# Seven buffers in place of three for the embedding terms of the gate

## The chip, the core and the metric

The kernel runs on one core of a Trainium2 chip. The core has a matrix engine (TensorE, PE in the profile; its weight loads are PEld), a vector engine (VectorE, DVE), an activation engine (ScalarE, ACT), a general engine (GpSimd, POOL) and a queue engine (SyncE, SP), which here issues the DMA transfers. Each engine works through its instructions in the order in which they are written for it, and semaphores hold an instruction until what it needs is there. SBUF is the on-chip memory for tiles, PSUM the memory (in banks) that TensorE writes. The metric is the time of one execution in microseconds; lower is better.

## What is computed

One layer of a hybrid encoder on 1024 positions of width 1024. The part around the change is the end of it:

```python
mixed = jnp.concatenate([attn, conv_out], axis=-1) @ w_out[i]
x = x + rms_norm(mixed, post_norm_gain[i])
e = rms_norm(p[i] @ w_ple_proj[i], ple_norm_gain[i])
x = x + jax.nn.sigmoid(x @ w_ple_gate[i]) * e
```

`attn` is block-causal differential attention in four heads, `conv_out` a gated short convolution; both come from one projection of the normalised input.

## The kernel before

All activations lie transposed, as tiles of 128 channels by 512 positions: `kt` or `m` counts the 8 channel tiles, `n` the two halves of the positions. Each product is done in three passes of split operands (a high and a low part, lines 100 to 102), so that a tile of the output projection or the gate takes 8 x 3 = 24 matmuls of 512 columns.

The products e = p @ w_ple_proj are made at the start and stored to DRAM (`e_dram`). Projections, attention heads and convolutions follow. The last stage works on `mT` (the split copy of the concatenated result) with the 8 tiles of `w_out`, then on `x1` (the split copy of the new residual) with the 8 tiles of `w_gate`. A weight tile is loaded (`load_w`, line 124), cast by ScalarE into its high part and reduced by GpSimd to its low part (both in `split`, lines 89 and 90; the GpSimd instruction is called a split below). `out_half(m, n)` makes one tile of the output projection, and ScalarE copies it and squares it; VectorE adds the squares (line 523). `post` scales the result and adds x. `gate_half(m, n)` makes one tile of the gate. It loads the tile of e (line 550), scales it by gain and norm (line 551), takes tanh of the matmul result (line 560), and VectorE joins both in two instructions (lines 561 and 562) that write into the buffer of e. That buffer is then stored to the output (line 563). The last call, (7,1), does its matmuls and what follows in two pieces of 256 columns.

The gate's 16 tiles are made in the order (0,0) to (5,0), (0,1) to (5,1), (6,0), (6,1), (7,0), (7,1), written (m,n). The buffers of e come from the pool `c4` under the tag `e`. A buffer can be loaded again when the store that reads it has landed. Results of TensorE go to banks from two groups in turn, `p` with two banks and `s` with three.

The order on each engine is made by a scheduler when the kernel is built, from the program's text, its dependencies and its buffers. The pools of the last stage lie in memory that the stages before have left, so a larger pool also moves its neighbours, and what a tile of the last stage waits for can change with its place. The pool `c4` is opened before `wp2`, which holds five of the eight weight tiles.

The last projection tile of the convolutions (`pj`, emptied by lines 424 and 432) comes just before the output projection; line 427 and 428 finish the convolution's gate, line 287 a head's result.

Of the kernel before, what the change touches and what calls it, by code (L numbers as in the profile page):

```python
# [12 lines left out]
F32 = mybir.dt.float32  # L13
# [7 lines left out]
P = 128  # L21
# [4 lines left out]
HALF = 512  # L26
# [17 lines left out]
def hybrid_layer(ctx, tc, xT, pT, w_in, small, lams, w_out, w_ple, w_gate, outT):  # L44
# [18 lines left out]
    def bank_s(name):  # L63
        return ps_s.tile([P, HALF], F32, tag="s", bufs=3, name=name)

    def bank_p(name):
        return ps_s.tile([P, HALF], F32, tag="p", bufs=2, name=name)
# [16 lines left out]
    def col(base, k):  # L84
        return sm[:, base + k:base + k + 1]

    def split(hi, lo, src, scale=None, lo_eng=None):
        if scale is None:
            A.copy(out=hi, in_=src)  # L89
            (lo_eng or V).tensor_tensor(out=lo, in0=src, in1=hi.bitcast(F32), op=sub)  # L90
        else:
            return (A.activation(out=hi, in_=src, func=AF.Copy, scale=scale),
                    V.scalar_tensor_tensor(out=lo, in0=src, scalar=scale, in1=hi.bitcast(F32), op0=mult, op1=sub))

    def rsqrt(out, ssq, n, eps):
        V.tensor_scalar(out=out, in0=ssq, scalar1=1.0 / n, scalar2=eps, op0=mult, op1=add)
        G.tensor_tensor(out=out, in0=out, in1=nhalf[:, :ssq.shape[-1]], op=ALU.pow)
# [7 lines left out]
    def column_sums(acc, pool, extra=None, tag="flip"):  # L105
        flip = pool.tile([P, HALF], F32, tag=tag, name="flip")
        V.transpose(out=flip, in_=acc)
        part = tiny.tile([P, 32], F32, tag="part", name="part")
        V.tensor_reduce(out=part[:, 0:16], in_=flip.rearrange("p (f r) -> p f r", r=32), axis=AX.X, op=add)
        if extra is not None:  # L110
            V.tensor_tensor(out=part[:, 16:32].rearrange("p (t f) -> p t f", t=4),
                            in0=extra.unsqueeze(2).broadcast_to([P, 4, 4]),
                            in1=own.unsqueeze(1).broadcast_to([P, 4, 4]), op=mult)
        n = 16 if extra is None else 32
        ms = bank_t("ms")
        T.matmul(out=ms[:, :n], lhsT=fold, rhs=part[:, :n], start=True, stop=True)
        return ms

    def spread(out, row):
        V.transpose(out=out, in_=row.unsqueeze(2).broadcast_to([P, 16, 32]))  # L120

    def load_w(src, pool=None, lo_eng=G):
        raw = rawp.tile([P, KT, P], F32, tag="raw", name="raw")
        nc.sync.dma_start(out=raw, in_=src)
        w = (pool or wp).tile([P, 2, KT, P], F32R, tag="w", name="w")
        split(w[:, 0], w[:, 1], raw, lo_eng=lo_eng)
        return w

    def product(w, rhs, n, bank):
        for kt in range(KT):  # L130
            b = rhs[n][kt]
            mm3(bank, w[:, 0, kt], w[:, 1, kt], b[:, 0], b[:, 1], kt == 0, kt == KT - 1)
        return bank

    def operand(name):
        return [[hp.tile([P, 2, HALF], F32R, tag="H", name=f"{name}{n}_{kt}") for kt in range(KT)] for n in range(2)]
# [349 lines left out]
    with ExitStack() as st:  # L486
        cp = st.enter_context(tc.tile_pool(name="cp", bufs=1, reuse_waits="tile"))
        c2 = st.enter_context(tc.tile_pool(name="c2", bufs=2, reuse_waits="tile"))
        c4 = st.enter_context(tc.tile_pool(name="c4", bufs=4, reuse_waits="tile"))
        wp2 = st.enter_context(tc.tile_pool(name="wp2", bufs=5, reuse_waits="tile"))  # L490

        order = [(w_out, m) for m in range(KT)] + [(w_gate, m) for m in range(KT)]
        tiles = {}

        def weight(k):
            if k not in tiles:
                src, m = order[k]
                tiles[k] = load_w(src[m], pool=wp if k % KT in (1, 4, 7) else wp2)
            return tiles[k]

        banks = [0]

        def bank():
            banks[0] += 1
            return bank_p("o") if banks[0] % 2 else bank_s("o")

        mT = operand("mT")
        for n in range(2):
            for kt in range(KT):
                split(mT[n][kt][:, 0], mT[n][kt][:, 1], mix[kt][n])  # L510

        accs = [None, None]

        def out_half(m, n):
            ps = product(weight(m), mT, n, bank())
            A.copy(out=mix[m][n], in_=ps)
            if m == 0:
                accs[n] = cp.tile([P, HALF], F32, name=f"acc{n}")
                A.activation(out=accs[n], in_=ps, func=AF.Square)
            else:  # L520
                sq = c2.tile([P, HALF], F32, tag="sq", name="sqo")
                A.activation(out=sq, in_=ps, func=AF.Square)
                V.tensor_tensor(out=accs[n], in0=accs[n], in1=sq, op=add)

        x1 = None

        def post_stat(n):
            r = tiny.tile([P, 16], F32, tag="rs", name="rso")
            rsqrt(r, column_sums(accs[n], cp)[:, :16], D, 1e-6)
            return r  # L530

        def post(n, r):
            S1 = accs[n]
            spread(S1, r)
            for kt in range(KT):
                o = mix[kt][n]
                xt = c4.tile([P, HALF], F32, tag="xt", bufs=3, name="xt")
                nc.sync.dma_start(out=xt, in_=xT[n, kt])
                V.scalar_tensor_tensor(out=o, in0=o, scalar=col(C_POST, kt), in1=S1, op0=mult, op1=mult)  # L539
                (G if kt else V).tensor_tensor(out=o, in0=o, in1=xt, op=add)  # L540
                split(x1[n][kt][:, 0], x1[n][kt][:, 1], o)

        re = []

        def gate_half(m, n):
            if len(re) == n:
                re.append(cp.tile([P, HALF], F32, name=f"re{n}"))
                spread(re[n], rs_e[:, 16 * n:16 * n + 16])
            e = c4.tile([P, HALF], F32, tag="e", bufs=3, name="e")
            nc.sync.dma_start(out=e, in_=e_dram[n, m])  # L550
            V.scalar_tensor_tensor(out=e, in0=e, scalar=col(C_PLE, m), in1=re[n], op0=mult, op1=mult)  # L551
            w = weight(KT + m)
            pieces = 2 if (m, n) == (KT - 1, 1) else 1
            step = HALF // pieces
            for c0 in range(0, HALF, step):
                c, o = slice(c0, c0 + step), slice(n * HALF + c0, n * HALF + c0 + step)
                ps = bank()[:, :step]
                product(w, [[b[:, :, c] for b in r] for r in x1], n, ps)
                t = c2.tile([P, HALF], F32, tag="tg", name="tg")[:, :step]
                A.activation(out=t, in_=ps, func=AF.Tanh, scale=0.5)  # L560
                V.scalar_tensor_tensor(out=e[:, c], in0=t, scalar=1.0, in1=e[:, c], op0=add, op1=mult)
                V.tensor_tensor(out=e[:, c], in0=e[:, c], in1=mix[m][n][:, c], op=add)
                nc.sync.dma_start(out=outT[m * P:(m + 1) * P, o], in_=e[:, c])

        for m in range(KT):
            out_half(m, 0)
        r = post_stat(0)
        out_half(0, 1)
        x1 = operand("x1")
        post(0, r)  # L570
        for m in range(1, KT):
            out_half(m, 1)
        r = post_stat(1)
        gate_half(0, 0)
        post(1, r)
        for m in range(1, 6):
            gate_half(m, 0)
        for m in range(0, 6):
            gate_half(m, 1)
        for m in range(6, 8):  # L580
            gate_half(m, 0)
            gate_half(m, 1)
# [37 lines left out]
```

## Time and profile before

| | |
|---|---|
| median of 3 runs | 652.25 us (650.86 to 652.95) |
| the profiled execution | 651.04 us |
| its span in the trace | 649.3 us |
| VectorE busy | 447.8 us, 69% of the span |
| ScalarE busy | 243.7 us, 38% |
| GpSimd busy | 227.0 us, 35% |

The span runs from the first to the last profiled instruction of one execution. The executions shown differ among themselves by up to 2.1 us. Times in the trace count from the span's start.

### The profile page before, as it was taken

To read this page: it belongs to the slowest core of one execution; us is meant where nothing else is said; L and a number is where in the kernel's file an instruction comes from. 1 tells how busy PE (TensorE), PEld (TensorE's weight loads), DVE (VectorE), ACT (ScalarE), POOL (GpSimd) and SP (SyncE) were. 2 spreads that over 40 slices of the span, in tenths; PEclk is the share of its full clock that TensorE was granted. 3 is DMA by queue.
4 is the path that set the end of the run, shared out by engine and by line. 5 is a ranking of instruction groups with operands and counts; after the bars stand their busy time and mean duration, and the time that the engine had idled before them with its cause. 6 is when DMAs were issued, how large, how long until landed. Compare 5 with 4: busy or idle time off the path is not lost.

```text
span 649.3 us, 8064 instructions
## 1 busy us (share of the span) xinstructions
PE 631.8 (97%) x2941; PEld 523.2 (81%) x2941; DVE 447.8 (69%) x821; ACT 243.7 (38%) x442; POOL 227.0 (35%) x114
## 2 busy tenths in 40 slices
PE   7899999999999999999999999999999999999992
PEld 4688888888888888888888888888888888888882
DVE  6968512698786687876886999539881199795233
ACT  6945312334463333543444434114632326231110
POOL 2006100325326544256362132424560379450000
PEclk9999999999999999999999999999999999999997
DMA  8976522310254102352012400113140125143222
GB/s 286 383 279 194 195 86 86 92 58 5 82 145 138 44 34 81 103 158 65 33 49 82 130 33 33 65 34 130 65 163 0 34 73 187 33 145 98 93 86 97
DMA packets 35654, 67.77 MB, mean 104 GB/s; under 512 B 3744, under 2 KB 12448, under 8 KB 35616
## 3 DMA queue, kind: packets, MB, share of 16 engines
q1 hardware_dynamic: 35616, 67.27, 31.5%
q8 instruction: 23, 0.38, 0.2%
q14 instruction: 15, 0.12, 0.1%
HBM read 48.38 MB, written 12.58 MB: 94 GB/s over the span
## 4 chain that ended last, share of the span: by engine, by line
PE 71%; DVE 12%; DMA 9%; ACT 3%; issue 2%; POOL 2%; DVEq 0%; POOLq 0%; ACTq 0%
PE pj L100 14%; PE pj L102 14%; PE pj L101 14%; PE s L237 5%; DMA e<-e_dram 4%; DMA out_dram<-e 3%; DVE mix L539 3%; PE o L102 3%; PE o L100 3%; PE o L101 3%; PE tpw L264 2%; PE v L100 2%; PE v L101 2%; PE v L102 2%; DVE x L90 2%
## 5 line engine op out<-in xcount | busy, mean ns | idle before, releaser
L100 PE MATMUL pj<-hT,w 128*128 128x512 f32 x448 | 176.4, 394 | 1.2 <-ACT w L89 1.2
L101 PE MATMUL pj<-hT,w 128*128 128x512 f32 x448 | 176.2, 393 | 0.0
L102 PE MATMUL pj<-hT,w 128*128 128x512 f32 x448 | 176.1, 393 | 0.0
L90 POOL TENSOR_TENSOR w<-raw,w 128x1024 fp32r<-128x1024 f32 x41 | 105.5, 2582 | 146.6 <-ACT w L89 143.8
L100 PEld LDWEIGHTS pj<-hT,w 128*128 128x128 f32 x448 | 84.2, 188 | 18.1 <-ACT w L89 2.0
L102 PEld LDWEIGHTS pj<-hT,w 128*128 128x128 f32 x448 | 84.2, 188 | 16.4
L101 PEld LDWEIGHTS pj<-hT,w 128*128 128x128 f32 x448 | 84.2, 188 | 16.1
L245 ACT ACTIVATE p<-p,nm 128x128 f32<-128x128 f32 (+7 forms) x64 | 49.4, 772 | 70.6 <-DVE nm L241 60.7
L89 ACT CAST w<-raw 128x1024 fp32r<-128x1024 f32 x44 | 45.9, 1048 | 21.2 <-issue 11.6
L102 PE MATMUL o<-x,w 128*128 128x512 f32 (+1 forms) x136 | 51.3, 377 | 0.0
L100 PE MATMUL o<-x,w 128*128 128x512 f32 (+1 forms) x136 | 51.2, 377 | 0.0
L101 PE MATMUL o<-x,w 128*128 128x512 f32 (+1 forms) x136 | 51.2, 377 | 0.0
L100 PE MATMUL o<-mT,w 128*128 128x512 f32 x128 | 49.8, 389 | 0.0
L101 PE MATMUL o<-mT,w 128*128 128x512 f32 x128 | 49.8, 389 | 0.0
L102 PE MATMUL o<-mT,w 128*128 128x512 f32 x128 | 49.7, 390 | 0.0
L237 PE MATMUL s<-ks,qs 128*128 128x512 f32 (+2 forms) x192 | 47.5, 346 | 0.0
L89 ACT CAST wt<-tpw 128x512 fp32r<-128x512 f32 (+3 forms) x48 | 21.1, 479 | 60.1 <-PE tpw L264 60.0
L90 DVE TENSOR_TENSOR wt<-tpw,wt 128x512 fp32r<-128x512 f32 (+3 forms) x48 | 25.3, 551 | 26.2 <-ACT wt L89 26.1
L551 DVE SCALAR_TENSOR_TENSOR e<-e,small_c,re 128x512 f32<-128x512 f32 x16 | 16.3, 1017 | 36.5 <-DMA e<-e_dram 36.5
L241 DVE CUSTOM_DVE_ANT_0 p<-s,bias 128x512 f32<-128x512 f32 (+3 forms) x64 | 34.8, 564 | 9.3 <-PE s L237 5.4
L237 PEld LDWEIGHTS s<-ks,qs 128*128 128x128 f32 x192 | 33.4, 188 | 5.0
L405 POOL TENSOR_TENSOR mix<-mix,R 128x512 f32<-128x512 f32 x8 | 12.3, 1543 | 68.6 <-DVE mix L404 66.4
(139 smaller groups left out, 1117.6 us busy)
## 6 DMA issues: line engine op xcount, KB each, us to landing
raw<-in_w_in SPq DMA_DIRECT2D x32, 512.0 KB, 3.6
mix<-in_xT SPq DMA_DIRECT2D x16, 256.0 KB, 6.6
e_dram<-e SPq DMA_DIRECT2D x16, 256.0 KB, 5.6
mix<-e_dram SPq DMA_DIRECT2D x16, 256.0 KB, 3.1
ks<-ks SPq DMA_DIRECT2D x16, 256.0 KB, 3.5
v_dram<-v SPq DMA_DIRECT2D x8, 512.0 KB, 2.6
vs<-v_dram SPq DMA_DIRECT2D x32, 128.0 KB, 2.7
raw<-in_w_out SPq DMA_DIRECT2D x8, 512.0 KB, 3.2
```

The source lines that it names most:

```text
L89: A.copy(out=hi, in_=src)
L90: (lo_eng or V).tensor_tensor(out=lo, in0=src, in1=hi.bitcast(F32), op=sub)
L100: T.matmul(out=ps, lhsT=ah, rhs=bh, start=first, stop=False)
L101: T.matmul(out=ps, lhsT=ah, rhs=bl, start=False, stop=False)
L102: T.matmul(out=ps, lhsT=al, rhs=bh, start=False, stop=last)
L237: T.matmul(out=banks[m][:, :nn], lhsT=s.qs[:, m, qi], rhs=s.ks[:, m, part, c], start=part == 0, stop=part == 1)
L241: V.tensor_tensor_reduce(out=pr[m][:, c0:c0 + n], in0=banks[m][:, :n], in1=s.bias[:, b0:b0 + n], scale=-1.0, scalar=low[m], op0=add, op1=A ...
L245: A.activation(out=pr[m][:, :W], in_=pr[m][:, :W], func=AF.Exp, scale=-1.0, bias=low[m], accum_out=l[:, m:m + 1])
L264: T.transpose(out=tp[:, ii * P:(ii + 1) * P], in_=s.ws[ii][:, j * P:(j + 1) * P], identity=ident)
L405: G.tensor_tensor(out=o, in0=o, in1=R[n], op=mult)
L539: V.scalar_tensor_tensor(out=o, in0=o, scalar=col(C_POST, kt), in1=S1, op0=mult, op1=mult)
L551: V.scalar_tensor_tensor(out=e, in0=e, scalar=col(C_PLE, m), in1=re[n], op0=mult, op1=mult)
```

## The change

The pool's tag `e` gets seven buffers of 128 x 512 in place of three. Nothing is added or taken out; the built program has the same instructions in another order.

```diff
--- before.py
+++ after.py
@@ -546,7 +546,7 @@
             if len(re) == n:
                 re.append(cp.tile([P, HALF], F32, name=f"re{n}"))
                 spread(re[n], rs_e[:, 16 * n:16 * n + 16])
-            e = c4.tile([P, HALF], F32, tag="e", bufs=3, name="e")
+            e = c4.tile([P, HALF], F32, tag="e", bufs=7, name="e")
             nc.sync.dma_start(out=e, in_=e_dram[n, m])
             V.scalar_tensor_tensor(out=e, in0=e, scalar=col(C_PLE, m), in1=re[n], op0=mult, op1=mult)
             w = weight(KT + m)
```

What the scheduler makes of it shows at two places. The first is where the last stage begins. On VectorE the subtractions `mT1_k` (the low parts of the second half of mT) are line 90, line 432 empties the last projection tile `pj`, and the `e` tiles are e_4765 for (0,0), e_4852 for (1,0) and so on. Lines with - are of before, with + of the changed program:

```order
 L90 TENSOR_TENSOR mT1_3_4141<-mix3_1_117,mT1_3_4141 128x512
+L90 TENSOR_TENSOR mT1_4_4142<-mix4_1_119,mT1_4_4142 128x512
+L90 TENSOR_TENSOR mT1_5_4143<-mix5_1_121,mT1_5_4143 128x512
 L432 TENSOR_TENSOR mix7_1_125<-pj_4087,mix7_1_125 128x512
-L90 TENSOR_TENSOR mT1_4_4142<-mix4_1_119,mT1_4_4142 128x512
-L551 SCALAR_TENSOR_TENSOR e_4765<-e_4765,small_c_78,re0_4763 128x512
-L90 TENSOR_TENSOR mT1_5_4143<-mix5_1_121,mT1_5_4143 128x512
-L551 SCALAR_TENSOR_TENSOR e_4852<-e_4852,small_c_78,re0_4763 128x512
 L90 TENSOR_TENSOR mT1_6_4144<-mix6_1_123,mT1_6_4144 128x512
 L90 TENSOR_TENSOR mT1_7_4145<-mix7_1_125,mT1_7_4145 128x512
```

Two subtractions move ahead of line 432, and the scalings of line 551, which stood between them, move behind the last of the subtractions, where there are now six in a row. On ScalarE at the same place, w_4180, w_4247 and w_4281 are the high parts of w_out's tiles 0, 2 and 3, and line 425 is the tanh of the last convolution gate:

```order
 L89 CAST mT0_7_4137<-mix7_0_124 128x512
+L89 CAST w_4180<-raw_4178 128x1024
+L89 CAST w_4247<-raw_4245 128x1024
+L89 CAST w_4281<-raw_4279 128x1024
 L425 ACTIVATE ty_4081<-y_4080 128x512
 L89 CAST mT1_0_4138<-mix0_1_111 128x512
```

These three casts stood behind mT1_3 before. A little later on ScalarE, w_4315, w_4349 and w_4383 are the tiles 4, 5 and 6, and lines 516 and 519 copy and square the first tile of the output projection:

```order
 L89 CAST mT1_5_4143<-mix5_1_121 128x512
+L89 CAST w_4315<-raw_4313 128x1024
 L89 CAST mT1_6_4144<-mix6_1_123 128x512
+L89 CAST w_4349<-raw_4347 128x1024
 L89 CAST mT1_7_4145<-mix7_1_125 128x512
-L89 CAST w_4315<-raw_4313 128x1024
+L516 COPY mix0_0_110<-o_4183 128x512
+L519 ACTIVATE acc0_4209<-o_4183 128x512
+L89 CAST w_4383<-raw_4381 128x1024
```

Two casts have moved ahead of the cast of mT1_7, and that of w_4383 stands behind it.

The second place is the gate, here on VectorE: e_5143 is (3,1), e_5176 is (4,1), e_5209 is (5,1), e_5242 is (6,0), e_5280 is (6,1) and e_5351 is (7,1), the last tile:

```order
 L561 SCALAR_TENSOR_TENSOR e_5143<-tg_5171,e_5143 128x512
-L551 SCALAR_TENSOR_TENSOR e_5209<-e_5209,small_c_78,re1_5042 128x512
+L551 SCALAR_TENSOR_TENSOR e_5351<-e_5351,small_c_78,re1_5042 128x512
 L562 TENSOR_TENSOR e_5143<-e_5143,mix3_1_117 128x512
 L561 SCALAR_TENSOR_TENSOR e_5176<-tg_5204,e_5176 128x512
-L551 SCALAR_TENSOR_TENSOR e_5242<-e_5242,small_c_78,re0_4763 128x512
 L562 TENSOR_TENSOR e_5176<-e_5176,mix4_1_119 128x512
 L561 SCALAR_TENSOR_TENSOR e_5209<-tg_5237,e_5209 128x512
-L551 SCALAR_TENSOR_TENSOR e_5280<-e_5280,small_c_78,re1_5042 128x512
 L562 TENSOR_TENSOR e_5209<-e_5209,mix5_1_121 128x512
```

Line 551 still stands between lines 561 and 562 of another tile, but for a tile further ahead, and behind (3,1) there is none left. On SyncE at that point, where e_5110 is (2,1):

```order
 L563 DMA out_0_dram<-e_5110 128x512
-L550 DMA e_5209<-e_dram_93 128x512
+L550 DMA e_5351<-e_dram_93 128x512
 L563 DMA out_0_dram<-e_5143 128x512
-L550 DMA e_5242<-e_dram_93 128x512
 L563 DMA out_0_dram<-e_5176 128x512
-L550 DMA e_5280<-e_dram_93 128x512
 L563 DMA out_0_dram<-e_5209 128x512
```

The last load follows the store of (2,1), and from there on only stores are left.

## Rows read from the trace of the kernel before

**Rows 1.** The page: span; busy time, share and instructions of each engine.

```profile
span 649.3 us, 8064 instructions
...
PE 631.8 (97%) x2941; PEld 523.2 (81%) x2941; DVE 447.8 (69%) x821; ACT 243.7 (38%) x442; POOL 227.0 (35%) x114
```

**Rows 2.** By stretches: busy us (count) of PE, PEld, DVE, ACT, POOL; clock; DMA share; GB/s.

```profile
600.00:620.00 20.00, 20.00 (x90) 16.57 (x89) 7.28 (x12) 1.80 (x3) 0.00 (x0) 1.00 0.24 80
```

**Rows 3.** Timeline of the end: start, duration in us, engine, line, operation.

```profile
631.37 0.39 PE L102 MATMUL o<-x,w 128*128 128x512 f32 x1
...
637.23 0.28 PE L102 MATMUL o<-x,w 128*128 128x256 f32 x1
637.80 0.38 ACT L560 ACTIVATE tg<-o 128x256 f32<-128x256 f32 x1 [5.40 <-DVE e L561]
...
645.19 0.42 DVE L561 SCALAR_TENSOR_TENSOR e<-tg,e 128x256 f32<-128x256 f32 x1
645.64 0.42 DVE L562 TENSOR_TENSOR e<-e,mix 128x256 f32<-128x256 f32 x1
```

**Rows 4.** Chain that ended last, 636 to 650 us: start, duration, what.

```profile
637.13 1.99 DMA out_dram<-e
...
639.13 2.54 DMA e<-e_dram
```

**Rows 5.** Source view of line 551: idle VectorE before it (us, times).

```profile
  DMA e<-e_dram: 36.5, 11
```

**Rows 6.** Timeline of VectorE in the gate stage; idle time before in brackets.

```profile
599.46 0.75 DVE L551 SCALAR_TENSOR_TENSOR e<-e,small_c,re 128x512 f32<-128x512 f32 x1 [2.93 <-DMA e<-e_dram]
...
617.71 0.75 DVE L551 SCALAR_TENSOR_TENSOR e<-e,small_c,re 128x512 f32<-128x512 f32 x1 [4.18 <-DMA e<-e_dram]
618.37 0.69 DVE L562 TENSOR_TENSOR e<-e,mix 128x512 f32<-128x512 f32 x1
```

**Rows 7.** Timeline of ScalarE in the gate stage.

```profile
615.48 0.60 ACT L560 ACTIVATE tg<-o 128x512 f32<-128x512 f32 x1 [4.84 <-PE o L102]
620.91 0.60 ACT L560 ACTIVATE tg<-o 128x512 f32<-128x512 f32 x1 [4.84 <-PE o L102]
...
631.79 0.60 ACT L560 ACTIVATE tg<-o 128x512 f32<-128x512 f32 x1 [4.84 <-PE o L102]
```

**Rows 8.** DMA issues: tensors, KB each, median us from issue to landing.

```profile
raw<-in_w_out SPq DMA_DIRECT2D x8, 512.0 KB, 3.2
...
e<-e_dram SPq DMA_DIRECT2D x16, 256.0 KB, 2.6
```

**Rows 9.** Timelines of ScalarE, GpSimd, VectorE at the entry; GpSimd's splits grouped.

```profile
454.10 0.63 ACT L89 CAST mT<-mix 128x512 fp32r<-128x512 f32 x1 [2.38 <-DVE mix L432]
458.01 0.63 ACT L425 ACTIVATE ty<-y 128x512 f32<-128x512 f32 x1 [3.28 <-DVE y L424]
...
461.15 2.00 ACT L89 CAST w<-raw 128x1024 fp32r<-128x1024 f32 x2
...
462.27 2.41 POOL L90 TENSOR_TENSOR w<-raw,w 128x1024 fp32r<-128x1024 f32 x1 [9.77 <-ACT w L89]
...
L90 POOL TENSOR_TENSOR w<-raw,w 128x1024 fp32r<-128x1024 f32 x7 | 18.8, 2723 | 9.8 <-ACT w L89 9.8
...
458.67 0.69 DVE L427 SCALAR_TENSOR_TENSOR ty<-ty,y 128x512 f32<-128x512 f32 x1 [0.76 <-ACT ty L425]
...
460.49 1.89 DVE L90 TENSOR_TENSOR mT<-mix,mT 128x512 fp32r<-128x512 f32 x3
...
463.34 0.69 DVE L432 TENSOR_TENSOR mix<-pj,mix 128x512 f32<-128x512 f32 x1 [0.97 <-PE pj L102]
...
467.52 2.88 DVE L551 SCALAR_TENSOR_TENSOR e<-e,small_c,re 128x512 f32<-128x512 f32 x1
470.33 2.88 DVE L90 TENSOR_TENSOR mT<-mix,mT 128x512 fp32r<-128x512 f32 x1
```

**Rows 10.** Timeline of TensorE: first matmul after the last projection tile.

```profile
463.14 0.39 PE L100 MATMUL o<-mT,w 128*128 128x512 f32 x1
```

## Prediction

> **What bounds the kernel now.** I read the page first [rows 1]: TensorE is busy for 97% of the span. So a change can gain only where TensorE waits, or after it has finished. The table by stretches [rows 2] shows no such wait: from 600 to 620 us TensorE is busy for all of the 20.00 us, at a granted clock of 1.00, the level of 2.4 GHz. In order of time the last matmul starts at 637.23 us and takes 0.28 [rows 3]; the span ends at 649.3. Between lie 11.8 us in which TensorE has nothing to do. The chain of waits, read from that side [rows 4], tells what fills them: a store, 1.99, and the load that waits for it, 2.54. Behind the load come the scaling of line 551, lines 562 and 561, and then the next store: one turn of a loop. The source view of line 551 [rows 5] prices its wait at 36.5 us over 11 of 16 tiles. VectorE's own order of time [rows 6] gives its period: line 551 starts at 599.46 and, three turns later, at 617.71, 6.08 us apart, while TensorE feeds tanh (line 560) every 5.43 us [rows 7]. So VectorE falls further behind with each tile. TensorE never feels it (it has free banks), but after its last matmul VectorE still has tiles (6,1), (7,0) and (7,1) to finish. Most of the 36.5 us are therefore worth nothing; only what is left after 637.5 us counts.
>
> **The change part by part: the end.** With seven buffers the load for tile k waits for the store of tile k-7. That alone would free every load, but VectorE works in the order written: line 551 of a later tile still stands between lines 561 and 562 of the current one, and its load stands on SyncE behind the store of the tile before. So the old loop goes on, with its 6.08 us, for as long as there are tiles left to load. The order of the changed program shows where that ends: the last line 551, of (7,1), now stands ahead of line 562 of (3,1), where before it was that of (5,1). In the trace this place is passed at 617.71 [rows 6]. From there on no load is left. VectorE ends (3,1) at 619.0 and needs lines 561 and 562 alone for each further tile, 0.61 + 0.61 = 1.2 us. The tanh of (5,1) started at 615.48, that of (6,0) at 620.91, ending at 621.51 [rows 7]; that of (4,1) came before both. (4,1) ends at 620.2, (5,1) at 621.5: VectorE has caught up at (6,0), three tiles before the end, and from then on waits for TensorE.
>
> The end is then one short chain behind the last matmul. It ends at 637.23 + 0.28 = 637.51. An activation that waits for matmuls alone starts 0.03 after them (the L102 of 631.37 ends at 631.76, tanh starts at 631.79) [rows 3, 7]. Tanh of 512 columns takes 0.60 there; for the last tile's 256 I take the 0.38 of [rows 3]: 637.92. Line 561 follows at 637.95 (line 427 started 0.03 after its tanh [rows 9]), line 562 0.45 later, as 645.64 followed 645.19: 638.40. In the trace this last line 562 starts at 645.64 [rows 3]. What comes after it, 649.3 - 645.64 = 3.66 us, is the last store and the finish, and stays. **Saved: 7.24 us.** A store lands in 1.99 [rows 4], so of these 3.66 no more than 1 can be the crowd of the last stores; I take none of it, and 0.5 for the range.
>
> **The entry of the last stage.** The larger pool also moves other tiles, and the order changes around 455 to 485 us. Three weight casts of ScalarE go ahead of line 425, into a gap of 3.28 us that ScalarE has there [rows 9]; three casts at some 0.95 fill it without making line 425 late. So GpSimd's splits (line 90, w), which began at 462.27 after 9.77 idle, begin at 454.10 + 0.63 + 1.05, about 455.8. That helps nobody, since TensorE did not wait for weights. What it may cost is on VectorE. Beside a split, a VectorE operation on two SBUF tiles takes 2.88 us in place of 0.69, and they come 2.81 apart, one for each split; line 432, which reads PSUM, still takes 0.69 beside one [rows 9]. Now the splits lie beside operations that had been free of them, and two more subtractions (mT1_4, mT1_5) go ahead of line 432. TensorE waits for that line: the tile m = 2 takes the bank that it empties. TensorE gets there after tiles 0 and 1, whose remaining 45 matmuls start at 463.14 [rows 10], at 5.43/24 = 0.226 each: 473.3.
>
> When is line 432 done? Before it stand, from 455.79 on, lines 287, 427, 428 and the subtractions mT1_0 to mT1_5. The sixth split's cast (w_4383) now stands on ScalarE behind the cast of mT1_7, which needs line 432's result, so no more than five splits come before it. The first takes 2.41, the next four 2.81 each: they end near 469.5 (the weight loads of 3.2 us [rows 8] are issued as the first and second split end, in time). One operation passes per split: 287, 427, mT1_0, 428, mT1_1, the last done near 470.1. Four subtractions at 0.6 (three start within 1.89 [rows 9]) and line 432 at 0.69 bring 473.1 or so, just ahead of 473.3. I take **a cost of 0**, with bounds of 0 and one more period, 2.8.
>
> By the Trainium skill (SBUF — State Buffer, section SBUF: two separate sides) VectorE and GpSimd share a port pair as an exclusive lock, and a VectorE instruction with two SBUF inputs blocks for the whole GpSimd instruction that reads SBUF. By that rule five blocked operations cost the same 473.1; the trace agrees, 2.88 beside a split against 0.69 for the line that reads PSUM.
>
> The other moves cost nothing, each by its cover. Seven operations of line 551 now stand ahead of most of line 523. At worst each takes 2.81 from 474.6, so the sums start up to 20 us later, near 494. ScalarE, with two buffers for squares, would then stop at the tile m = 3, and TensorE would want the bank of m = 4 only when m = 7 ends, 473.3 + 6 x 5.43 = 505.9: 11 us of cover. Without it the excess would be added to the span. The loads of e, 2.6 us each [rows 8], are issued near 461 to 470 and needed from 474.6; one of them waits on SyncE for line 428 (near 467), and the weight load behind it is not cast before 477 anyway. From 505 to 590 the order differs only in which e tile line 551 names.
>
> **The sum.** 649.3 - 7.2 + 0 = 642.1 us of span. The profiled execution lay 651.04 - 649.3 = 1.74 above its span, which gives 643.8. It was 1.2 below the median of the three runs, 652.25, which on the same count gives 645.0. I forecast a median between them, 644.4.
>
> **Rivals.** (a) *The ports undo it.* If splits run without a break from 458.7, each of the eight operations 427, 428 and mT1_0 to mT1_5 takes 2.81: line 432 is done at 458.67 + 22.5 + 0.69 = 481.9, TensorE stops for 8.6 us, and 643.8 + 8.6 = 652.4, slower than before by 1.4 on the profiled basis. It decides from line 432 later than 480.5 on. For it: from 462.3 on the trace shows such a run, seven splits in 18.8 us [rows 9]. Against it: five splits at most can come first. The smaller form, one period or two lost, gives 646.6 to 649.4. (b) *The loads stay in the loop.* If VectorE were not to catch up after (3,1), the end would keep its 3 tiles of lag and the time would be 651 to 652. For it: four tiles, (0,1) to (3,1), still wait for the store of the tile before. Against it: no load is left after them, and 1.2 us of work stands against 5.43 per tile. (c) *The end is not the loop*, and a store or the finish takes as long anyway: 651. The chain of waits [rows 4] speaks against it, with 4.5 of each 6.08 us in the two transfers.
>
> **Numbers.** The forecast, with a gain of 5 to 8.5 us, has 0.80; the smaller form of (a) 0.12; (a) in full 0.04; (b) and (c) together 0.04. The range is 642.8 (profiled basis, with 0.5 of stores and 0.5 of scatter) to 647.4 (median basis with most of one lost period). 0.3%, 2 us, is about what can be told from no change. Faster by more: 0.92, the forecast and the smaller form; same: 0.05, from (b), (c) and the milder half of (a); slower: 0.03.
>
> **What would show it.** After: the last matmul within 0.5 us of 637.5 and the last line 562 within 1.5 us behind it; line 551's wait at less than half of 36.5 us, with none after about 618; line 561 waiting for tanh for the last three tiles. At the entry: splits from 456, line 432 near 473, and no idle TensorE. The prediction is wrong if TensorE shows a gap near 473 or its last matmul ends past 639, or if VectorE still waits for e after 625.

## The result, and the profile after

The changed kernel takes 644.38 us (median of 4 runs, 643.67 to 644.88), the kernel before 652.1 on the same chip. The ratio is 0.9882, with a 95% interval of 0.9863 to 0.9902: 7.7 us less. The profiled execution of after took 644.88 us; its span is 643.1.

One thing first, to read its times rightly. In this execution all of the last stage lies 0.92 us later than in that of before, and it did so ahead of anything that the change touches: the first matmul of the output projection starts at 457.95, against 457.02, and the same lag stands from 304 us on. So a time of before plus 0.92 is the same place, and a time of after less 0.92 is called below a time on the clock of before.

Two lines of the page of after, the span with the busy time of each engine [rows 1], and the engines' shares of the chain that ended last:

```profile
span 643.1 us, 8064 instructions
...
PE 634.9 (99%) x2941; PEld 525.6 (82%) x2941; DVE 448.1 (70%) x821; ACT 242.7 (38%) x442; POOL 227.7 (35%) x114
...
PE 91%; ACT 3%; DMA 2%; POOL 2%; DVE 1%; issue 1%; SPq 0%; POOLq 0%; ACTq 0%
```

TensorE is busy for 99% of the span, and the chain runs through it almost alone. The table by stretches of after shows it as full between 600 and 620 us as [rows 2] did, with a granted clock of 1.00:

```profile
600.00:620.00 20.00, 20.00 (x90) 16.58 (x89) 7.32 (x12) 2.39 (x4) 0.00 (x0) 1.00 0.24 79
```

The source view of line 551 in after, its idle time before the load of e and how often [rows 5]:

```profile
  DMA e<-e_dram: 20.2, 7
```

The timeline of the gate stage in after: VectorE [rows 6, 3], then ScalarE [rows 7] (start, duration, engine, line, operation; in brackets the idle time before, and what ended it).

```profile
600.70 0.68 DVE L562 TENSOR_TENSOR e<-e,mix 128x512 f32<-128x512 f32 x1
...
612.38 0.75 DVE L551 SCALAR_TENSOR_TENSOR e<-e,small_c,re 128x512 f32<-128x512 f32 x1 [4.24 <-DMA e<-e_dram]
...
618.55 0.75 DVE L551 SCALAR_TENSOR_TENSOR e<-e,small_c,re 128x512 f32<-128x512 f32 x1 [4.21 <-DMA e<-e_dram]
619.22 0.68 DVE L562 TENSOR_TENSOR e<-e,mix 128x512 f32<-128x512 f32 x1
619.82 0.68 DVE L561 SCALAR_TENSOR_TENSOR e<-tg,e 128x512 f32<-128x512 f32 x1
620.53 0.69 DVE L562 TENSOR_TENSOR e<-e,mix 128x512 f32<-128x512 f32 x1
621.14 0.69 DVE L561 SCALAR_TENSOR_TENSOR e<-tg,e 128x512 f32<-128x512 f32 x1
621.86 0.69 DVE L562 TENSOR_TENSOR e<-e,mix 128x512 f32<-128x512 f32 x1
622.47 0.69 DVE L561 SCALAR_TENSOR_TENSOR e<-tg,e 128x512 f32<-128x512 f32 x1
623.20 0.69 DVE L562 TENSOR_TENSOR e<-e,mix 128x512 f32<-128x512 f32 x1
627.91 0.69 DVE L561 SCALAR_TENSOR_TENSOR e<-tg,e 128x512 f32<-128x512 f32 x1 [4.02 <-ACT tg L560]
...
638.88 0.43 DVE L561 SCALAR_TENSOR_TENSOR e<-tg,e 128x256 f32<-128x256 f32 x1 [1.99 <-ACT tg L560]
639.35 0.43 DVE L562 TENSOR_TENSOR e<-e,mix 128x256 f32<-128x256 f32 x1
...
589.42 0.60 ACT L560 ACTIVATE tg<-o 128x512 f32<-128x512 f32 x1 [3.73 <-DVE e L561]
...
605.52 0.60 ACT L560 ACTIVATE tg<-o 128x512 f32<-128x512 f32 x1 [4.84 <-PE o L102]
...
621.84 0.60 ACT L560 ACTIVATE tg<-o 128x512 f32<-128x512 f32 x1 [4.84 <-DVE e L561]
```

Up to 618.55 VectorE goes round the old loop, one turn in 6.2 us, and waits 4.2 us in each for a load of e. The line 551 at 618.55 is the last. Behind it (3,1) ends, and (4,1), (5,1) and (6,0) follow 1.3 us apart, with no wait. At 622.47 line 561 of (6,0) meets its tanh, which started at 621.84: VectorE has caught up, and from 627.91 on it waits for tanh. The last line 562 starts 0.9 us behind the last matmul (638.15 to 638.43), where before it was 8.1 us behind.

The entry, in the timeline of after [rows 9, 10]: VectorE, GpSimd, and the matmul of TensorE that first writes the bank that line 432 empties.

```profile
456.71 2.92 DVE L287 SCALAR_TENSOR_TENSOR mix<-flipa,small_c,mix 128x512 f32<-128x512 f32 x1
459.56 0.68 DVE L424 TENSOR_TENSOR y<-pj,R 128x512 f32<-128x512 f32 x1
...
465.19 2.89 DVE L428 SCALAR_TENSOR_TENSOR mix<-ty,mix 128x512 f32<-128x512 f32 x1
468.00 5.29 DVE L90 TENSOR_TENSOR mT<-mix,mT 128x512 fp32r<-128x512 f32 x5
473.21 0.68 DVE L432 TENSOR_TENSOR mix<-pj,mix 128x512 f32<-128x512 f32 x1
...
456.67 8.04 POOL L90 TENSOR_TENSOR w<-raw,w 128x1024 fp32r<-128x1024 f32 x3 [3.24 <-ACT w L89]
465.10 5.23 POOL L90 TENSOR_TENSOR w<-raw,w 128x1024 fp32r<-128x1024 f32 x2 [0.39 <-ACT w L89]
476.54 5.79 POOL L90 TENSOR_TENSOR w<-raw,w 128x1024 fp32r<-128x1024 f32 x2 [6.21 <-ACT w L89]
...
474.27 0.39 PE L100 MATMUL o<-mT,w 128*128 128x512 f32 x1
```

Five splits come ahead of line 432 and none more; a VectorE operation on two SBUF tiles beside a split takes 2.9 us, and line 432 ends at 473.89. TensorE comes to the tile that needs its bank at 474.27 (473.3 + 0.92 = 474.2 by the prediction), and has no gap there: less than 0.4 us of room.

### The profile page after: what moved, and what is told of

It reads as the page before. It is cut to its first block, busy times and chain, and to the rows that moved or that the text cites. A ratio compares the mean times of both kernels' runs of the same rounds, so it can differ in the third digit from the quotient of the medians.

```text
span 643.1 us, 8064 instructions
## 1 busy us (share of the span) xinstructions
PE 634.9 (99%) x2941; PEld 525.6 (82%) x2941; DVE 448.1 (70%) x821; ACT 242.7 (38%) x442; POOL 227.7 (35%) x114
## 4 chain that ended last, share of the span: by engine, by line
PE 91%; ACT 3%; DMA 2%; POOL 2%; DVE 1%; issue 1%; SPq 0%; POOLq 0%; ACTq 0%
PE pj L100 15%; PE pj L102 15%; PE pj L101 14%; PE o L102 9%; PE o L100 9%; PE o L101 9%; PE s L237 5%; PE tpw L264 2%; PE v L101 2%; PE v L102 2%; PE v L100 2%; PE av L102 1%; PE av L101 1%; PE av L100 1%; POOL mix L442 1%; DMA rawe<-in_w_ple 1%
## 5 line engine op out<-in xcount | busy, mean ns | idle before, releaser
L253 DVE SCALAR_TENSOR_TENSOR p<-p,rl,p 128x128 f32<-128x128 f32 (+7 forms) x32 | 32.7, 1021 | 0.4
```

The lines of the kernel that those rows point to most:

```text
L253: V.scalar_tensor_tensor(out=pr[0][:, :W], in0=pr[1][:, :W], scalar=rl, in1=pr[0][:, :W], op0=mult, op1=add)
```

## The experiments

Each ratio is to the kernel before on the same chip, with its 95% interval. There were three chips: beside the runs with four and five buffers, 1,192 columns and three buffers with the stored tile apart the kernel before took 651.5 us, beside the run with four buffers and the stored tile apart 651.6, and beside the others 651.7. The changed kernel was set against 652.1, so a difference between a run and the changed kernel, given below from the medians, comes out up to 0.9 us larger by the ratios. Times in the traces are compared with those of before as they stand, unless it is said otherwise: the last stage begins within 0.4 us of the same place.

### Four and five buffers

```diff
-            e = c4.tile([P, HALF], F32, tag="e", bufs=3, name="e")
+            e = c4.tile([P, HALF], F32, tag="e", bufs=4, name="e")
```

> Four buffers for e. Theory of the loop: the last line 551, of (7,1), stands ahead of line 562 of (6,0), three turns later than with seven, so VectorE leaves the loop at 617.71 + 3 x 6.08 = 635.96 (on the clock of the kernel before) and then does (6,0), (6,1), (7,0) and the two halves of (7,1) without a break: the last line 562 starts near 641.0 instead of 645.64 or 638.40. Time 652.1 - 4.6 = 647.5 or 644.4 + 2.6 = 647.0. The entry of the stage keeps the order of the kernel before. Rival, each added buffer gives an equal share of the 7.7 us: 650.2.

The second has `bufs=5`.

> Five buffers for e. Theory of the loop: the last line 551 stands ahead of line 562 of (5,1), so VectorE leaves the loop near 629.9 and has (6,0), (6,1) and (7,0) done near 634.8, before the last tile's tanh: nothing of the lag is left at the end, and the time is that of seven buffers, 644.4. The entry is that of seven buffers. Rival, each buffer gives an equal share: 648.2.

Four buffers took 646.68 us (ratio 0.9929, 0.9910 to 0.9948), five 643.99 (0.9889, 0.9868 to 0.9911). VectorE's timeline, first with four, then with five:

```profile
635.70 0.75 DVE L551 SCALAR_TENSOR_TENSOR e<-e,small_c,re 128x512 f32<-128x512 f32 x1 [4.29 <-DMA e<-e_dram]
...
640.87 0.42 DVE L562 TENSOR_TENSOR e<-e,mix 128x256 f32<-128x256 f32 x1
```

```profile
630.02 0.75 DVE L551 SCALAR_TENSOR_TENSOR e<-e,small_c,re 128x512 f32<-128x512 f32 x1 [4.22 <-DMA e<-e_dram]
...
637.88 0.43 DVE L561 SCALAR_TENSOR_TENSOR e<-tg,e 128x256 f32<-128x256 f32 x1 [1.73 <-ACT tg L560]
638.34 0.42 DVE L562 TENSOR_TENSOR e<-e,mix 128x256 f32<-128x256 f32 x1
```

The place of the last line 551 decides, as worked out: passed at 635.70 (635.96 expected), the rest doesn't fit in front of the last tanh, and the last line 562 starts at 640.87 (641.0 expected). Passed at 630.02 (629.9 expected), it fits, and line 561 waits for tanh again. Equal shares (650.2 and 648.2) lie far off. Two of the four added buffers bring all of the gain, as far as the two intervals can tell.

### The larger pool alone

```diff
-            e = c4.tile([P, HALF], F32, tag="e", bufs=3, name="e")
+            e = c4.tile([P, 1192], F32, tag="e", bufs=3, name="e")[:, :HALF]
```

> Three buffers for e, each as large as 2.3 of them, so that the pool is as large as with seven: weight casts, splits and line 432 move at the entry as with seven buffers, and the loads of e still wait for the stores. Theory of the loop: 652.1, as before, with line 551 waiting some 36 us for e, and no idle TensorE near 474. Rival, part of the gain comes from the other order at the entry: less than 650. Rival, the entry costs time that the gain hides: above 654.

It took 652.88 us (1.0022, 1.0011 to 1.0034): neither a share of the gain nor the 654 of the rival, but slower by more than the interval. The wait of line 551 was there as expected (37.3 us), and the entry had no gap; yet the last matmul came at 640.26, 3.2 us later than before when both are counted from the first matmul of the output projection. TensorE lost it bit by bit: from the 460s on many matmuls of 512 columns started 0.234 us apart in place of 0.227. No more than 1.4 us of it show in the time, since VectorE still ends last here, its last line 562 at 647.28. I put the loss down to my size of 1,192 columns. Three buffers of 4,768 bytes are 14,304, which is 223 x 64 + 32, so that the five weight tiles of `wp2`, the pool behind, start 32 bytes off a multiple of 64. With 1,280 columns they don't (15,360 = 240 x 64):

```diff
-            e = c4.tile([P, HALF], F32, tag="e", bufs=3, name="e")
+            e = c4.tile([P, 1280], F32, tag="e", bufs=3, name="e")[:, :HALF]
```

> As the run with three large buffers before it (4,768 bytes each a partition), but of 5,120 bytes each, so that the pools behind start at a multiple of 64 bytes again; there the weights of five tiles in eight had started 32 bytes off one, and the matmuls of the last two stages lay up to 0.234 us apart in place of 0.227. Theory (the entry's new order costs nothing, and the addresses made that run slower): last matmul within 0.5 us of 637.2, spacing 0.227 throughout, time as before, 651.5. Rival (the larger pool or its order slows TensorE): last matmul near 640, time near 652.9 again.

651.15 us (0.9988, 0.9977 to 1.0000), last matmul at 637.33, spacing 0.227 throughout. Its entry is that of seven buffers, five splits and all, with line 432 at 472.41 to 473.09 on a clock 0.1 us from that of before, and TensorE lost nothing by it. So the new order of the entry, by itself, neither gains nor costs.

### The address alone

```diff
-            e = c4.tile([P, HALF], F32, tag="e", bufs=7, name="e")
+            e = c4.tile([P, 520], F32, tag="e", bufs=7, name="e")[:, :HALF]
```

> Seven buffers of 2,080 bytes a partition in place of 2,048 (the last 32 bytes are unused), every instruction in the same order; the five weight tiles of the pool behind them then start 32 bytes off a multiple of 64. Theory of the addresses: matmuls that use these weights lie 0.231 to 0.234 us apart in place of 0.227, as in the run with 4,768 bytes, the last matmul comes some 3 us later, and as TensorE sets the end here, all of it counts: 647.2. Rival, the addresses mean nothing: 644.2.

646.94 us (0.9926, 0.9907 to 0.9944), 2.6 us above seven plain buffers, with the last matmul at 640.49, again 3.2 us later from the same start. (Seven buffers of 2,080 bytes are 14,560, or 227 x 64 + 32.) The table by stretches shows TensorE as full as ever, at the same clock, but with 88 matmuls in 20 us in place of 90:

```profile
600.00:620.00 20.00, 20.00 (x88) 16.22 (x87) 7.42 (x12) 2.40 (x4) 0.00 (x0) 1.00 0.24 79
```

From TensorE's timeline of the same run, three matmuls of a tile whose weights lie in the pool `wp`, in front of e, and three of one with weights in `wp2`:

```profile
609.89 0.39 PE L100 MATMUL o<-x,w 128*128 128x512 f32 x1
610.12 0.39 PE L101 MATMUL o<-x,w 128*128 128x512 f32 x1
610.35 0.39 PE L102 MATMUL o<-x,w 128*128 128x512 f32 x1
...
616.12 0.40 PE L100 MATMUL o<-x,w 128*128 128x512 f32 x1
616.36 0.39 PE L101 MATMUL o<-x,w 128*128 128x512 f32 x1
616.59 0.40 PE L102 MATMUL o<-x,w 128*128 128x512 f32 x1
```

The first three start 0.23 apart, two steps in 0.46; the others two steps in 0.47. Over 24 matmuls it is 0.2267 against 0.2333. The slow and fast stretches follow the weight tiles one by one: (1,0), (4,0), (1,1), (4,1) and (7,0), whose weights are in `wp`, run at 0.2267 (but for one stop in (1,0), for two small matmuls of line 116, which the kernel before has too), and the gate tiles of 512 columns between them at 0.2333. The 20 of the stage's 32 tiles whose weights lie in `wp2` make up the whole loss: 20 x 24 x 0.0067 = 3.2 us.

### The stored tile apart

```diff
-                V.tensor_tensor(out=e[:, c], in0=e[:, c], in1=mix[m][n][:, c], op=add)
-                nc.sync.dma_start(out=outT[m * P:(m + 1) * P, o], in_=e[:, c])
+                y = c4.tile([P, HALF], F32, tag="y", bufs=3, name="y")[:, :step]
+                V.tensor_tensor(out=y, in0=e[:, c], in1=mix[m][n][:, c], op=add)
+                nc.sync.dma_start(out=outT[m * P:(m + 1) * P, o], in_=y)
```

Here line 563 of the profile is what line 562 is elsewhere, and line 564 the store.

> Three buffers for e, but line 562 writes another tile (three buffers of its own), which is stored, so that an e buffer is free as soon as line 562 has read it and no load waits for a store. Theory of the loop: a turn loses the store's 2 us and is near 4.1 us, under TensorE's 5.43, so VectorE keeps up with three buffers: 644.4, as with seven. Rival, three loads ahead are too few however they are freed, or the load of 2.6 us alone holds VectorE back: 649 to 652.

647.03 us (0.9929, 0.9912 to 0.9946): a miss of 2.6 us, between the theory and the rival. The chain of waits shows a turn of the loop (start, duration, what):

```profile
614.84 0.70 DVE y L563
...
615.56 0.34 SPq L564
...
615.95 3.00 DMA e<-e_dram
...
619.04 0.10 DVE e L551
...
619.71 0.70 DVE e L561
...
620.43 0.70 DVE y L563
```

The turn takes 5.59 us, not 4.1; the others take 5.3 to 5.6, but for one of 7.1. I had left out that the load stands on SyncE behind the issue of the store, 0.39, and that beside a store it takes 2.7 to 3.0 (once 4.55). The rows show a third term: line 561 lies in the turn, 0.7, since line 551 of a later tile stands here ahead of lines 561 and 563 of the current one, where in before it stands between lines 561 and 562. So the turn is about TensorE's 5.43, and VectorE stays as late as it was. How late that is, VectorE's timeline of this run shows: line 563 of (0,1) starts at 598.93 and that of (3,1) at 614.84; the tanh of the two ends at 588.91 and 605.23. It is 10.0 us late at the first tile of the second half, and 9.6 three tiles later. The next run is made from that.

The same with four e buffers (`bufs=4`):

> Four e buffers, and the stored tile apart (three buffers of its own). Theory after the run with three of each: VectorE is some 10 us late when it comes to the second half's tiles (after the work of 564 to 588 us), and a loop that has the load alone in it turns in 5.3 to 5.6 us, about TensorE's 5.43, so it keeps that lag and doesn't work it off; what ends the lag is leaving the loop. With four buffers the last line 551 stands ahead of line 561 of (6,0), one turn earlier, passed near 631.5 to 632 (the run with three had one load of 4.55 us; without it 630.5): (6,0), (6,1), (7,0) are done by 636.5, before the last tile's tanh at 637.9, and the time is that of seven buffers, 644.4. Four buffers without the split gave 646.7. Rival, the loop's speed sets the end, whatever the place where it is left: 646 to 647, as with three.

643.54 us (0.9870, 0.9847 to 0.9894). VectorE's timeline:

```profile
625.80 0.75 DVE L551 SCALAR_TENSOR_TENSOR e<-e,small_c,re 128x512 f32<-128x512 f32 x1 [4.55 <-DMA e<-e_dram]
...
631.43 0.75 DVE L551 SCALAR_TENSOR_TENSOR e<-e,small_c,re 128x512 f32<-128x512 f32 x1 [3.55 <-DMA e<-e_dram]
...
635.48 0.69 DVE L563 TENSOR_TENSOR y<-e,mix 128x512 f32<-128x512 f32 x1
...
637.63 0.42 DVE L561 SCALAR_TENSOR_TENSOR e<-tg,e 128x256 f32<-128x256 f32 x1 [0.67 <-ACT tg L560]
```

The loop is no faster than with three (5.63 us from 625.80 to 631.43), and the gain is there all the same, since it is left one turn earlier. The interval of the ratio holds those of five and of seven buffers, so these runs don't tell the three apart.

### The room at the entry

Three VectorE operations that change nothing stand ahead of line 432 of the last projection tile, with seven buffers and then with three.

```diff
             def ev_b(s, n, ps):
-                o = mix[s.kt][n]
+                o = mix[s.kt][n]; [V.tensor_tensor(out=o, in0=o, in1=o, op=ALU.max) for _ in range(3 if (s.kt, n) == (7, 1) else 0)]
```

> Seven buffers, and three more VectorE operations (a maximum of a tile with itself, which changes nothing) ahead of line 432 of the last projection tile; the order puts one subtraction (mT1_6) ahead of it too. Theory: line 432 was done 0.3 us before TensorE needs its bank; four operations at 0.62 put it off by 2.5, so TensorE stops for 2.2 us near 474, and the last matmul and the end move by as much: 644.2 + 2.2 = 646.4. Rival, the bank is not what TensorE needs there, or there is more room than 0.3 us: no gap, 644.2.

> The same three operations in the kernel with three buffers. Theory: there the splits start only at 462.3, line 432 was done at 464.0 and has 9.3 us of room; up to three of the operations ahead of it are held by a split, 2.81 each, so it ends near 471, still before 473.3: no idle TensorE, time as before, 651.5, and in the worst case (four held) 0.5 us. So the same work is free in the one order and costs 2.2 us in the other. Rival, the extra operations cost the same in both: 653.7.

With seven buffers 647.06 us (0.9927, 0.9907 to 0.9948), 2.7 above the same without them; with three 652.37 (1.0006, 0.9993 to 1.0019), no change. TensorE's and VectorE's timeline with seven:

```profile
473.11 0.39 PE L102 MATMUL o<-mT,w 128*128 128x512 f32 x1
...
474.90 0.69 DVE L432 TENSOR_TENSOR mix<-pj,mix 128x512 f32<-128x512 f32 x1
...
475.73 0.47 PE L100 MATMUL o<-mT,w 128*128 128x512 f32 x1 [2.23 <-DVE mix L432]
```

The next matmul starts 2.62 us after the one before instead of 0.23, so 2.4 are lost, and the profile names line 432. With three buffers the same line ran at 467.96, on a clock 1.5 us behind that of before, and TensorE had no gap. Its end, 467.2 on the clock of before, is earlier than the 471 worked out, as a split held one of the added operations and not three. The rest came as expected: the change had used up 9 us of room and left less than 0.4.

## Why the prediction was right, step by step

**The end.** On the clock of before the last line 551 was passed at 617.6 (617.71 predicted), VectorE caught up at (6,0), and the last line 562 started at 638.43 (638.40). What stood behind it took 3.75 us instead of 3.66. So 7.1 us were saved in the profiled execution from the same place on, where 7.24 were predicted, and 7.7 of the medians. The mechanism and its size are as predicted. That the median met the forecast to 0.02 us is luck: executions of the changed kernel alone differ by 1.2.

One reason needs mending. The prediction said that VectorE falls further behind with each tile, by 6.08 - 5.43. That is true, and it is the smaller part of how late VectorE is. In after, line 562 of (0,1) starts at 600.70 behind a tanh that ended at 590.02, and that of (3,1) at 619.22 behind 606.12: 10.7 us late, then 13.1. In before VectorE goes on falling behind. The tanh of (0,1) and of (6,1) on ScalarE, and line 562 of the two on VectorE, in the timeline of before:

```profile
588.49 0.60 ACT L560 ACTIVATE tg<-o 128x512 f32<-128x512 f32 x1 [3.74 <-DVE e L561]
...
626.36 0.60 ACT L560 ACTIVATE tg<-o 128x512 f32<-128x512 f32 x1 [4.84 <-PE o L102]
...
600.12 0.69 DVE L562 TENSOR_TENSOR e<-e,mix 128x512 f32<-128x512 f32 x1
...
642.47 0.68 DVE L562 TENSOR_TENSOR e<-e,mix 128x512 f32<-128x512 f32 x1
```

VectorE is 11.0 us late at (0,1) and 15.5 at (6,1). Some 11 us were there before the second half began. VectorE has been busy until then with lines 539, 540 and 90 of the second half's operands, in after from 566 to 588, while the gate's first tiles wait; eight of line 539 alone take 9.5 us (timeline of after):

```profile
566.03 9.53 DVE L539 SCALAR_TENSOR_TENSOR mix<-mix,small_c,acc 128x512 f32<-128x512 f32 x8
```

So the loop harms twice. It adds 4.5 us, and it keeps VectorE from working off the 11, at some 4.1 us per tile (5.43 less the 1.3 that it needs for one), as it does in after once the loop is left: 13.1 us late at (3,1), 0.8 at (6,0). The two runs with the stored tile apart show both. With a loop at TensorE's pace nothing is added, and some 4.5 us of the 7.7 are gained; the rest comes with such a loop left one turn earlier.

**The entry.** The splits began at 455.75 on the clock of before (455.8), five came ahead of line 432, which ended at 472.97 (473.1), and TensorE had no gap (a cost of 0). With 0.2 us to spare by the prediction's own sum and a next step of 2.8, that no cost came of it is in part luck. By the Trainium skill (SBUF — State Buffer, section SBUF: two separate sides) a VectorE operation with two SBUF inputs is held for the whole of a GpSimd instruction that reads SBUF and has started first; the trace agrees again, 2.9 for line 287 beside a split against 0.68 for line 424, which reads PSUM and lies beside one too. Two details were off. Line 425 did come later, by 1.4 us, since line 287 was held ahead of the line 424 that it waits for. And the loads ahead were dearer than [rows 8] says: between 460 and 475 us those of e took 5.2 us (median) and those of `w_out` 5.5, with the DMA engines busy for 0.77 of the stretch from 457 to 475. They still came in time; VectorE did not wait for one.

**What was to show it.** The last matmul was due within 0.5 us of 637.5 and came at 637.51 on the clock of before; line 561 waits for tanh for the last three tiles. One mark was missed: line 551's wait came to 20.2 us, not under half of 36.5 (18.25). The four turns up to 618 make 15.8 us of it (3.2, then 4.2 each); I had not counted the three shorter waits ahead of them.

**The rivals.** (a) is real as a mechanism and less than 0.4 us short of a price, by the run with three more operations. (b) would have needed a loop that never ends; with four buffers it ends late, and 2.3 us of the gain are lost by the medians, 3.1 by the ratios. (c) fell with the last line 562. That the entry's new order brings the gain, which the prediction did not name, is ruled out by the run with 1,280 columns.

## What to carry to other kernels

A wait that is long in sum is worth what is left of it when the engine that sets the end is done: find the last instruction that waits, see what stands behind it on its engine, and count from there. A consumer that is late needs time without waits to catch up; a loop as fast as its producer only keeps it as late as it is. So the number of buffers counts by where it puts the last load, and past that point more of them bring nothing, as seven here bring no more than five. A larger pool moves its neighbours too: look at the order on each engine and at the room that it leaves, and at the addresses of what lies behind it.

## What the runs showed of the hardware

With weight tiles that start 32 bytes off a multiple of 64 matmuls of 512 columns lie 0.2333 us apart in place of 0.2267, 2.9% more, at a granted clock of 1.00, with TensorE shown as busy in both and the weight loads at 0.188 us in both. It cost 3.2 us of TensorE's time in each of two profiles, and 2.6 us of the median in the run where TensorE sets the end. The addresses are worked out from the sizes of the buffers, and that it is the reading of the weights from which tiles are slow; why it is so stays open, and other offsets than 32 bytes were not tried.
